# Input projection of a hybrid decoder layer on Trainium2: chunk-by-chunk start, paired chunk steps, conditioning by a pace per tile

## The chip, the core and the metric

The kernel runs on one core of one Trainium2 chip. A core has a matrix engine (PE, whose weight load is shown as PEld), a vector engine (DVE), a scalar engine (ACT), a general engine (POOL) and an engine whose queue issues nearly all transfers here (SP). The metric is the device time of one execution in microseconds (us): the median of three runs of the kernel before is 1449.34 us, the lowest 1449.11, the highest 1449.62. The profile is one further execution with its trace.

## The reference

One layer, one sequence of 256 positions, width 2048, all in 32-bit floats. A vector c conditions the layer: six vectors of 2048 (shift, scale and gate for each of two sub-layers) come from one product with a 2048 x 12288 matrix, `w_ada`.

```
c_act = silu(c)
mod = c_act @ w_ada + b_ada
sh1, sc1, g1, sh2, sc2, g2 = split(mod, 6)
h = layer_norm(x) * (1.0 + sc1) + sh1
y = token_mixer(h, w_in, ...)          # proj = h @ w_in, then attention and mLSTM
x = layer_norm(ALPHA * x + g1 * y, ...)
h = layer_norm(x) * (1.0 + sc2) + sh2
y = conv_ffn(h, w_up, ..., w_down)
x = layer_norm(ALPHA * x + g2 * y, ...)
```

Inside the token mixer one input projection `proj = h @ w_in` feeds two branches. One is a sparse attention with eight heads (compressed, selected and sliding-window keys, mixed by gates). The other is an mLSTM matrix memory with four heads, whose forget gates need a running maximum over all positions before it can start. Merge gates (another part of the projection, `mg`) mix the branches, an output projection follows, and then a gated feed-forward with a short convolution, which is most of the arithmetic. The change touches the layer norm and conditioning of x, the input projection, and the order of four small steps of the mLSTM and attention gates.

## The kernel before

**Products in three parts.** A 32-bit product is made of three products of a reduced type: the high part of both, and high by low in both orders. Every weight tile of 128 x 1024 floats (512 KB) is loaded by SP into one of 7 buffers `w`; ACT rounds it to its high part `wh` (L138), DVE subtracts to get the low part `wl` (L139), with 4 buffers each; then PE multiplies (L105). The activations are split in the same way into `hT` (high and low, L376 and L377).

**Row chunks and groups.** The 2048 rows of `w_in` are 16 row chunks k of 128, and PE accumulates over them in PSUM. They are taken in groups of 3, 4, 5 and 4 chunks. Within a group come first 24 blocks b of 128 columns (`ps_b`), then six column strips (`ps_a`, 392 or 512 wide). Eight of the blocks (0 to 7) stay in four PSUM banks over all groups; the others are added up in SBUF after each group. A weight tile holds 8 blocks of one chunk or two chunks of one strip, so a chunk takes six tiles and all 16 take 96. `order_b` gives the order of blocks and chunks within a group.

**Conditioning.** Chunk k can be used once its 128 shifts and scales are known: two dot products of 2048 with c, which DVE makes of transferred rows of `w_ada`, either one instruction of 128 x 2048 (L216, buffers `adaA`, `adaB`) or two of 128 x 1024 (L226, in `w` buffers), then two small additions into `modc` (L244, L245). Then ACT scales and shifts the normalised, transposed `nT` into `hm` (L374), casts `hT` high (L376), and DVE subtracts `hT` low (L377). A ticker hands out one conditioning product every few weight tiles, at a rate worked out per group so that the next group's chunks are through by then, and drains what is left at the group's end (`tk.drain`). Beyond the start, chunks are modulated two at a time.

**Startup.** x is normalised and transposed on PE (L353, `ps_nT`), ACT copies the transposes out of PSUM to `nT` (`turned`, L357), chunks 0 and 1 are conditioned together (`ada_mod(0, 2)`), then the first tile starts. Matmuls on zeros (L365, `ps_i`, 12 and then 4) stand among them on PE. DVE and ACT are ordered by hand in this part.

**Gate steps.** In the last group the generator `gate_steps` makes, step by step, the transposes and the small vector work for the branches: `ps_sT`, `ps_F`, `ps_uT` (L597, copied by DVE at L599, then a running maximum, the scan at L600, to `mT`), `ps_mc` (L604, transposes of `mT`), `ps_sc` (L615). Steps are taken between the tiles of strips 3 and 4 (at `(k - k0) % 2`, so four of them); what is left over is taken later in one go, in a block whose PE order is by hand and in which the matmuls of `ps_mg` stand before and after. All other order comes from a scheduler of the language that sets each engine's queue ahead of time; on the chip each engine works its queue in order.

Of the kernel before, what the change touches and what calls it, by code (L numbers as in the profile page):

```python
# [14 lines left out]
P = 128  # L15
# [17 lines left out]
GROUPS = (3, 4, 5, 4)  # L33
FIRST = 2
# [7 lines left out]
NIDLE = 12, 4  # L42
# [34 lines left out]
def build(ctx: ExitStack, tc: tile.TileContext, d, out, dbg=None):  # L77
# [54 lines left out]
    def load_split(src, off=0, t=None, after=()):  # L132

        n = src.shape[-1]
        if t is None:
            t = load(src)
        wh, wl = halves(off)
        hi = nc.scalar.copy(wh[:, :n], t[:, :n])  # L138
        lows.append(nc.vector.tensor_sub(wl[:, :n], t[:, :n], wh[:, :n]))  # L139
        for ins, other in zip((hi, lows[-1]), after):  # L140
            behind(ins, other)
        return wh, wl
# [56 lines left out]
    ring, cyclic, wide = [], [], []  # L199
# [33 lines left out]
    def ada_cols(m, n, k0, k1, then=None):  # L233
# [7 lines left out]
        def last():  # L241
# [3 lines left out]
            nc.vector.tensor_add(o, o, bada[:, m:m + n, k0:k1])  # L245
# [23 lines left out]
    class Ticker:  # L269
# [25 lines left out]
        def until(self, g):  # L295
            self.flush()
            while g in self.q:
                run_all(self.q.pop(0))
# [57 lines left out]
    def turned(p):  # L356
        return nc.scalar.copy(nT[:, 2 * p:2 * p + 2, :], psx.pop(p).rearrange("p (a b) -> p a b", a=2))  # L357
# [9 lines left out]
    def modulate_in(k0, k1):  # L367
        tmp = t2([P, 2, S], "hm")[:, :k1 - k0, :]
        for k in range(k0, k1):
            if k0 == 0:  # L370
                nc.vector.tensor_scalar(tmp[:, k - k0, :], nT[:, k, :], modc[:, 1, k:k + 1],
                                        modc[:, 0, k:k + 1], op0=ALU.mult, op1=ALU.add)
                continue
# [5 lines left out]
    mods = []  # L379

    def ada_mod(k0, k1):

        while k0 < k1:
            k = min(k0 + 2, k1)
            yield from ada_cols(0, 2, k0, k, lambda k0=k0, k=k: mods.append(modulate_in(k0, k)))
            k0 = k

    adaA = pg.tile([P, 2, D], F32, name="adaA", tag="gates0")
    ring += [None, None, adaA[:, 0, :]]
    zr = t2([P, 512], "zr", F32R)  # L390
    nc.gpsimd.memset(zr.bitcast(F32), 0.0)
    first = ada_mod(0, FIRST)
    idle(NIDLE[0], zr[:, :P], zr)
    with tc.manual_schedule(engines={mybir.EngineType.DVE, mybir.EngineType.Activation}):
# [6 lines left out]
        todo = [next(first) for _ in range(4)]  # L401
        tile0 = load(d["w_in_b"][0])
        steps = []
        for t in range(2):
            st = p0.tile([P, 4, 6], F32, name="st_x%d" % t, tag="st", bufs=2)
            for c in range(4):
                nc.vector.bn_stats(st[:, c, :], xt[:, t, c * 512:(c + 1) * 512])
                if t and c == 0:
# [3 lines left out]
                    for i in range(2):  # L412
# [4 lines left out]
        for i in range(2, 4):  # L417
            normalise(0, i)
# [3 lines left out]
        for f in todo[:1]:  # L422
            f()
# [3 lines left out]
        for f in todo[1:]:  # L427
            f()
        for c in range(2):
            normalise(1, c)  # L430
            for p in (2 * c, 2 * c + 1):
                turn(p, 1)
        turned(0)
        normalise(1, 2)
        turned(1)
        split0 = halves(OFFB[0])
        nc.scalar.copy(split0[0], tile0)
# [4 lines left out]
        for p in (2, 3):  # L442
            turned(p)
# [3 lines left out]
        for f in first:  # L447
            f()
        lows.append(nc.vector.tensor_sub(split0[1], tile0, split0[0]))
        for p in (4, 5):  # L450
            turned(p)

# [89 lines left out]
    def turn_rest():  # L542
        adaB = p0.tile([P, 2, D], F32, name="adaB", tag="t16")
        ring.extend([adaA[:, i, :] for i in range(2)] + [adaB[:, i, :] for i in range(2)])
        cyclic.append(1)
# [6 lines left out]
    def load_rest():  # L552
        nc.sync.dma_start(gb, d["ml_gate_b"][0:1, :].to_broadcast([P, 8]))
        nc.sync.dma_start(prm, d["prm"])
        msk = t2([P, P], "msk")
        nc.sync.dma_start(msk, d["msk"])
# [78 lines left out]
    def stream(src, width, per, off=0):  # L635

        for i in range(src.shape[0]):
# [3 lines left out]
            if n == 1:  # L641
                turn_rest()
            if n:
                t = load(cut, wide[-1] if n in (2, 3) else None)
                wh, wl = load_split(cut, off[i % 2], t, mods[n // 4] if n in (1, 4) else ())
                if n == 1:
                    for p in (6, 7):
                        turned(p)
            else:
                wh, wl = split0  # L650
            if n == 8:
                load_rest()
            if n in (1, 2):
                tk.tick(1.0)
                tk.flush()
            elif n:
                work()
            for i in range(per):
# [3 lines left out]
                                                           ("w_in_v", 512, 2, (0, 0))))  # L662
    k0 = 0
    lag = []
    for gi, kn in enumerate(GROUPS):
        nxt = gi < len(GROUPS) - 1
        if nxt:
            if gi == 0:
                tk.add(ada_mod(FIRST, kn))
            tk.add(ada_mod(k0 + kn, k0 + kn + GROUPS[gi + 1]))  # L670
            rate = 2 * GROUPS[gi + 1] / (6 * kn - (4 if gi == 0 else 2))
        else:
            rate = GR1
            ring.clear()
        comp = []

        def work():
# [3 lines left out]
            tk.tick(rate if nxt or c < 3 else GR2)  # L681

        c = 0
        for b, ks in order_b(gi):
# [870 lines left out]
```

## Time and profile before

| | |
|---|---|
| median of 3 runs | 1449.34 us (1449.11 to 1449.62) |
| profiled execution, its own time | 1448.23 us |
| its span, first to last instruction | 1446.3 us |
| mean granted PE clock | 0.994 |
| PE busy | 1418.9 us (98%) |
| DVE busy | 1061.5 us (73%) |
| ACT busy | 700.2 us (48%) |
| first matmul of each group | 25.02, 74.53, 140.64, 216.74 us |
| `ps_uT`, `ps_mc`, `ps_sc` | 293.47, 299.92, 300.13 us |

A row of the timeline gives the start, the time of the instructions in it, the engine, the line, the operation with its tiles, shapes, how many instructions the row joins, and in square brackets how long the engine was idle before and which instruction ended that. A row of the windows gives the stretch and its length, the busy time of PE, PEld, DVE, ACT and POOL in it with the number of instructions, the clock granted to PE as a share of full speed, the share of the transfer engines' time, and GB/s. A group row gives the number of instructions, their busy time, the mean ns of one, and the idle time before them.

### The profile page before, as it was taken

How to read it: one execution, taken by the hardware profiler on the slowest of the kernel's cores; microseconds unless marked ns; L12 is line 12 of the kernel's file. 1: busy time of each engine (PE TensorE's matmuls, PEld its weight loads, DVE VectorE, ACT ScalarE, POOL GpSimd, SP SyncE). 2: the span in 40 equal slices, each digit the busy share in tenths (PEclk: the TensorE clock that was granted, in tenths of full speed). 3: DMA queues.
4: the chain of work that ended last, by engine and by line, in shares of the span. 5: the costliest groups of instructions: out<-in, count | busy, mean ns of one | idle time of the engine just before them, and what ended most of it. 6: DMA issues, size and time to landing. Idle time of an engine off the chain costs nothing.

```text
span 1446.3 us, 23680 instructions
## 1 busy us (share of the span) xinstructions
PE 1418.9 (98%) x9361; PEld 1280.7 (89%) x9361; DVE 1061.5 (73%) x1486; ACT 700.2 (48%) x954; POOL 3.6 (0%) x10
## 2 busy tenths in 40 slices
PE   7999999999999999999999999999999999999996
PEld 6998998877777888888999999988889999998886
DVE  7889886888787898779878768755555555555566
ACT  5654344746566444445565454444334444444341
POOL 0000000000000000000000000000000000000000
PEclk8999999999999999999999999999999999999998
DMA  9999878886867999899188878866666666666661
GB/s 373 418 403 371 286 239 279 301 289 217 308 219 288 357 318 344 342 334 349 37 298 293 289 237 287 292 191 190 189 198 195 192 195 196 192 193 197 190 205 59
DMA packets 103183, 374.25 MB, mean 259 GB/s; under 512 B 11168, under 2 KB 11680, under 8 KB 102304
## 3 DMA queue, kind: packets, MB, share of 16 engines
q1 hardware_dynamic: 103072, 372.75, 75.3%
q8 instruction: 73, 1.20, 0.3%
q14 instruction: 38, 0.31, 0.1%
HBM read 370.61 MB, written 2.10 MB: 258 GB/s over the span
## 4 chain that ended last, share of the span: by engine, by line
PE 89%; DVE 6%; ACT 2%; issue 1%; DMA 1%; DVEq 0%
PE ps_up L105 33%; PE ps_d L105 17%; PE ps_mg L105 12%; PE ps_b L105 8%; PE ps_br L105 6%; PE ps_a L105 6%; PE ps_o L105 3%; DVE wl L139 2%; PE ps_s L105 1%; PE ps_y L105 1%; PE ps_hid L105 1%; DVE w L226 1%; DVE adaB L216 1%; DVE xz L1150 0%; DMA w<-in_w_o_dram 0%
## 5 line engine op out<-in xcount | busy, mean ns | idle before, releaser
L139 DVE TENSOR_TENSOR wl<-w,wh 128x1024 fp32r<-128x1024 f32 (+1 forms) x475 | 571.0, 1206 | 321.7 <-ACT wh L138 320.4
L138 ACT CAST wh<-w 128x1024 fp32r<-128x1024 f32 (+1 forms) x475 | 490.9, 1038 | 610.2 <-PE ps_up L105 184.9
L105 PE MATMUL ps_up<-h2T,wh 128*128 128x256 f32 x2816 | 480.9, 276 | 0.5 <-DVE h2T L1258 0.5
L105 PEld LDWEIGHTS ps_up<-h2T,wh 128*128 128x128 f32 x2816 | 424.4, 188 | 0.9 <-DVE h2T L1258 0.8
L105 PE MATMUL ps_up<-h2T,wl 128*128 128x256 f32 x1408 | 386.8, 276 | 0.0
L105 PEld LDWEIGHTS ps_up<-h2T,wl 128*128 128x128 f32 x1408 | 264.4, 188 | 0.0
L105 PE MATMUL ps_d<-wh,uTt 128*128 128x512 f32 (+1 forms) x704 | 205.6, 376 | 0.0
L105 PE MATMUL ps_mg<-wh,hT 128*128 128x512 f32 x512 | 169.2, 401 | 0.0
L226 DVE SCALAR_TENSOR_TENSOR w<-w,crow 128x1024 f32<-128x1024 f32 x134 | 163.0, 1219 | 3.0 <-ACT crow L197 3.0
L105 PEld LDWEIGHTS ps_d<-wh,uTt 128*128 128x128 f32 x704 | 129.2, 188 | 24.0
L105 PE MATMUL ps_b<-hT,wh 128*128 128x256 f32 x768 | 133.7, 282 | 1.5 <-ACT hT L376 1.2
L105 PE MATMUL ps_d<-wl,uTt 128*128 128x512 f32 (+1 forms) x352 | 132.2, 376 | 0.0
L105 PEld LDWEIGHTS ps_b<-hT,wh 128*128 128x128 f32 x768 | 115.6, 190 | 5.7 <-issue 3.3
L105 PEld LDWEIGHTS ps_mg<-wh,hT 128*128 128x128 f32 x512 | 96.2, 188 | 22.6 <-issue 3.1
L105 PE MATMUL ps_a<-wh,hT 128*128 128x392 f32 (+1 forms) x384 | 108.4, 359 | 0.0
L105 PE MATMUL ps_b<-hT,wl 128*128 128x256 f32 x384 | 101.2, 279 | 0.7 <-DVE wl L139 0.7
L105 PE MATMUL ps_mg<-wl,hT 128*128 128x512 f32 x256 | 100.0, 391 | 0.0
L105 PEld LDWEIGHTS ps_a<-wh,hT 128*128 128x128 f32 x384 | 70.8, 188 | 7.2 <-issue 2.1
L105 PEld LDWEIGHTS ps_d<-wl,uTt 128*128 128x128 f32 x352 | 66.1, 188 | 11.9
L105 PE MATMUL ps_a<-wl,hT 128*128 128x392 f32 (+1 forms) x192 | 69.6, 362 | 2.3 <-DVE wl L139 2.3
L105 PEld LDWEIGHTS ps_b<-hT,wl 128*128 128x128 f32 x384 | 69.7, 188 | 1.7 <-DVE wl L139 1.3
L105 PE MATMUL ps_o<-wh,mgT 128*128 128x512 f32 (+1 forms) x208 | 62.3, 381 | 0.0
(278 smaller groups left out, 1280.7 us busy)
## 6 DMA issues: line engine op xcount, KB each, us to landing
w<-in_w_up_dram SPq DMA_DIRECT2D x176, 512.0 KB, 4.3
w<-in_w_ada_dram SPq DMA_DIRECT2D x134, 512.0 KB, 4.7
w<-in_w_down_dram SPq DMA_DIRECT2D x89, 512.0 KB, 3.7
w<-in_w_mg_dram SPq DMA_DIRECT2D x64, 512.0 KB, 5.0
w<-in_w_in_b_dram SPq DMA_DIRECT2D x48, 512.0 KB, 7.0
w<-in_w_br_dram SPq DMA_DIRECT2D x32, 512.0 KB, 5.2
w<-in_w_o_dram SPq DMA_DIRECT2D x32, 512.0 KB, 5.4
adaA<-in_w_ada_dram SPq DMA_DIRECT2D x15, 1024.0 KB, 10.9
```

Of the source, the lines that this page charges most:

```text
L105: nc.tensor.matmul(o, lhsT, rhs, start=start, stop=stop)
L138: hi = nc.scalar.copy(wh[:, :n], t[:, :n])
L139: lows.append(nc.vector.tensor_sub(wl[:, :n], t[:, :n], wh[:, :n]))
L216: ins = nc.vector.scalar_tensor_tensor(t, t, 1.0, crow, op0=ALU.mult, op1=ALU.mult, accum_out=parts[:, row(m), k, 0:1])
L226: ins = nc.vector.scalar_tensor_tensor(t, t, 1.0, crow[:, i * 1024:(i + 1) * 1024], op0=ALU.mult, op1=ALU.mult, accum_out=parts[:, row(m), ...
```

## The change

- **Startup, chunk by chunk.** Chunk 0 is conditioned and modulated alone, straight out of PSUM by ACT (`modulate_one`), then chunk 1, then chunk 2. The first four weight tiles are opened by hand (`high`, `low`, `opened`): the order on PE is now written out too, with transposes of later chunks between the first tiles' matmuls. Nine instead of four idle matmuls stand before it.
- **Order of blocks.** Group 0 takes blocks 8 to 15 and 0 to 7 of chunk 0, the same of chunk 1, then of chunk 2. Later groups take the 16 blocks in steps of two chunks. Blocks 16 to 23 follow whole.
- **Conditioning.** One table `PACE` by the number of the tile gives the pace; nothing is drained at a group's end. Where a chunk is needed that isn't modulated yet, `need` forces what is queued.
- **Others.** The loads of three constants move from tile 8 to tile 46; the second ring buffer `adaB` is set up before the first group. In the last group the ring is cleared at block 3, not ahead of the group.
- **Gate steps.** They are taken in strips 3 and 4 at `(k - k0) % 3 == 2`: one per strip instead of two. The other three go to the block with the order by hand.

```diff
+PACE = ((26, 0.51), (42, 0.25), (50, 0.5), (72, 0.3), (96, 0.5))
-NIDLE = 12, 4
+NREST = 46
+NIDLE = 12, 9
...
-    if gi == len(GROUPS) - 1:
-        return [(b, range(kn)) for b in range(NBLK)]
-    most = 2 * HELD + (0 if gi else 8)
-    a, z = range(FIRST), range(FIRST, kn)
-    first = [*range(2 * HELD, most), *range(2 * HELD)]
-    return ([(b, a) for b in (range(most) if gi else first)] + [(b, z) for b in range(2 * HELD, most)]
-            + [(b, z) for b in range(2 * HELD)] + [(b, range(kn)) for b in range(most, NBLK)])
+    held, free = range(2 * HELD), range(2 * HELD, 2 * HELD + 8)
+    pairs = [range(k, min(k + 2, kn)) for k in range(0, kn, 2)]
+    if gi:
+        parts = [(ks, g) for ks in pairs for g in (held, free)]
+    else:
+        parts = [([k], g) for ks in ((0, 1), (2,)) for g in (free, held) for k in ks]
+    return [(b, ks) for ks, g in parts for b in g] + [(b, range(kn)) for b in range(16, NBLK)]
...
+        def force(self):
             self.flush()
-            while g in self.q:
-                run_all(self.q.pop(0))
+            f = next(self.q[0], 1)
+            if f == 1:
+                self.q.pop(0)
+            elif f:
+                f()
...
+    def modulate_one(k, src):
+        tmp = t2([P, S], "hm1")
+        for o in (hT[:, k, 0, :], tmp):
+            nc.scalar.activation(o, src, AF.Identity, bias=modc[:, 0, k:k + 1], scale=modc[:, 1, k:k + 1])
+        return lambda: nc.vector.tensor_sub(hT[:, k, 1, :], tmp, hT[:, k, 0, :])
...
+        todo[1]()
+        normalise(1, 0)
+        turn(0, 1)
+        late = modulate_one(0, psx[0][:, :S])
+        opened(0, 0, 8, 0, 0)
+        low(0)
+        late()
+        normalise(1, 1)
         turned(0)
+        opened(0, 0, 8, 1, 0)
+        opened(0, 0, 8, 0, 1)
+        for p in range(1, 4):
+            turn(p, 1)
+        sums[0]()
+        ring += adas
...
+        opened(1, 1, 8, 0, 0)
+        low(1)
+        later[0]()
+        high(2)
+        turned(3)
+        opened(1, 1, 8, 1, 0)
+        opened(1, 1, 8, 0, 1)
...
-            if n == 8:
+            if n == NREST:
                 load_rest()
...
+    def need(k):
+        while ready[-1] <= k:
+            tk.force()
...
-            rate = 2 * GROUPS[gi + 1] / (6 * kn - (4 if gi == 0 else 2))
-        else:
-            rate = GR1
-            ring.clear()
+        rate = None
...
-            tk.tick(rate if nxt or c < 3 else GR2)
+            pace = next(r for n, r in PACE if tiles[0] <= n)
+            tk.tick((rate or pace) if nxt or c < 3 else GR2)
...
             for k in ks:
+                need(k0 + k)
...
-                if not nxt and c in (3, 4) and (k - k0) % 2:
+                if not nxt and c in (3, 4) and (k - k0) % 3 == 2:
                     next(steps)
...
-        if nxt:
-            tk.drain()
```

In the order rows below a name after the operation is what is written and, behind the arrow, what is read; numbers at the end of a row count equal instructions in a row.

**PE at the start.** `ps_i` are the idle matmuls, `ps_nT` the transposes of x, `ps_b` the first blocks. Before:

```order
L365 MATMUL ps_i<-zr 128x512 x12
L353 MATMUL ps_nT<-head,xt 128x128 x8
L365 MATMUL ps_i<-zr 128x512 x4
L353 MATMUL ps_nT<-head,xt 128x128 x24
L105 MATMUL ps_b<-hT,wh 128x256 x16
L105 MATMUL ps_b<-hT,wl 128x256 x8
```

With the change:

```order
L372 MATMUL ps_i<-zr 128x512 x12
L358 MATMUL ps_nT<-head,xt 128x128 x8
L372 MATMUL ps_i<-zr 128x512 x9
L358 MATMUL ps_nT<-head,xt 128x128 x2
L107 MATMUL ps_b<-hT,wh 128x256 x8
L107 MATMUL ps_b<-hT,wl 128x256 x8
L107 MATMUL ps_b<-hT,wh 128x256 x8
L358 MATMUL ps_nT<-head,xt 128x128 x14
L107 MATMUL ps_b<-hT,wh 128x256 x8
L107 MATMUL ps_b<-hT,wl 128x256 x8
L107 MATMUL ps_b<-hT,wh 128x256 x8
L358 MATMUL ps_nT<-head,xt 128x128 x8
```

Ten transposes stand ahead of the first block instead of 32; the other 22 stand behind the first and the second tile.

**DVE in the same part, with the change,** from the last product of chunk 0 to the first of chunk 2 (`hm_229` and `hm_286` are chunks 0 and 1):

```order
L228 SCALAR_TENSOR_TENSOR w,parts<-w,crow 128x1024
L246 TENSOR_TENSOR modc<-parts 128x2
L247 TENSOR_TENSOR modc<-modc,head 128x2
L417 TENSOR_TENSOR wl<-w,wh 128x1024
L386 TENSOR_TENSOR hT<-hm_229,hT 128x256
L218 SCALAR_TENSOR_TENSOR adaA,parts<-adaA,crow 128x2048 x2
L246 TENSOR_TENSOR modc<-parts 128x2
L247 TENSOR_TENSOR modc<-modc,head 128x2
L417 TENSOR_TENSOR wl<-w,wh 128x1024
L386 TENSOR_TENSOR hT<-hm_286,hT 128x256
L218 SCALAR_TENSOR_TENSOR adaA,parts<-adaA,crow 128x2048
```

Each chunk has its own products, sums and low half here, and low halves of weight tiles stand between them; before, chunks 0 and 1 came together. Both products of chunk 1 are now 128 x 2048 and stand behind the low half of chunk 0. Chunk 2 follows in the same way, with the low halves of two tiles between its sums and its own low half.

**PE and DVE at the gate steps.** `ps_uT`, `ps_mc` and `ps_sc` are the three transposes, `ps_mg` the matmuls around them. PE with the change:

```order
L107 MATMUL ps_mg_3100<-wh,hT 128x512
L107 MATMUL ps_mg_3100<-wl,hT 128x512
L107 MATMUL ps_mg_3100<-wh,hT 128x512
L655 MATMUL ps_uT<-head,sm 4x128 x2
L662 MATMUL ps_mc<-head,mT 128x4 x2
L673 MATMUL ps_sc<-head,scT 128x128 x4
L107 MATMUL ps_mg_3099<-wh,hT 128x512
```

Before, three matmuls of `ps_a` and 24 of `ps_mg` stood between `ps_uT` and `ps_mc`; now none. DVE with the change, in the same place:

```order
L141 TENSOR_TENSOR wl<-w,wh 128x1024 x2
L228 SCALAR_TENSOR_TENSOR w,parts<-w,crow 128x1024
L657 COPY uT<-ps_uT 4x256
L141 TENSOR_TENSOR wl<-w,wh 128x1024
L228 SCALAR_TENSOR_TENSOR w,parts<-w,crow 128x1024
L658 SCALAR_TENSOR_TENSOR mT<-uT 4x256
```

One low half and one conditioning product stand between the copy of `uT` and the scan that makes `mT`, which the transposes into `ps_mc` read.

More of the change, by code (lines that the diff above doesn't have):

```diff
@@ L139, in load_split @@
         lows.append(nc.vector.tensor_sub(wl[:, :n], t[:, :n], wh[:, :n]))
-        for ins, other in zip((hi, lows[-1]), after):
-            behind(ins, other)
+        if after:
+            behind(lows[-1], after)
         return wh, wl
@@ L384, in ada_mod, with one_mod, high, low @@
             k = min(k0 + 2, k1)
-            yield from ada_cols(0, 2, k0, k, lambda k0=k0, k=k: mods.append(modulate_in(k0, k)))
+            yield from ada_cols(0, 2, k0, k, lambda k0=k0, k=k: (modulate_in(k0, k), ready.append(k)))
             k0 = k
     adaA = pg.tile([P, 2, D], F32, name="adaA", tag="gates0")
-    ring += [None, None, adaA[:, 0, :]]
+    adas = [adaA[:, i, :] for i in range(2)]
+    ring += [None, None, *adas]
     zr = t2([P, 512], "zr", F32R)
     nc.gpsimd.memset(zr.bitcast(F32), 0.0)
-    first = ada_mod(0, FIRST)
+    later = []
+    def one_mod(k, low=lambda f: f()):
+        yield from ada_cols(0, 2, k, k + 1, lambda: (low(modulate_one(k, nT[:, k, :])), ready.append(k + 1)))
+    first, second, third = ada_cols(0, 2, 0, 1), one_mod(1, later.append), one_mod(2)
+    splits = [halves(OFFB[i % 2]) for i in range(4)]
+    begun = [None] * 5
+    for j in range(HELD, HELD + 4):
+        psb[j] = bank(psm, "ps_b")
+    def high(n):
+        nc.scalar.copy(splits[n][0], begun[n])
+    def low(n):
+        lows.append(nc.vector.tensor_sub(splits[n][1], begun[n], splits[n][0]))
+    def opened(n, k, b0, w, x):
+        for i in range(8):
+            b = b0 + i
+            mm(psb[b // 2][:, (b % 2) * S:(b % 2 + 1) * S], splits[n][w][:, i * P:(i + 1) * P], hT[:, k, x, :],
+               not (k or w or x or b % 2), False)
     idle(NIDLE[0], zr[:, :P], zr)
-    with tc.manual_schedule(engines={mybir.EngineType.DVE, mybir.EngineType.Activation}):
+    with tc.manual_schedule(engines={mybir.EngineType.DVE, mybir.EngineType.Activation, mybir.EngineType.PE}):
         todo = [next(first) for _ in range(2)]
@@ L400, in build @@
             f()
-        todo = [next(first) for _ in range(4)]
-        tile0 = load(d["w_in_b"][0])
+        todo = [next(first) for _ in range(2)]
+        begun[0] = load(d["w_in_b"][0])
+        sums = [next(second) for _ in range(2)]
+        for n in range(1, 5):
+            begun[n] = load(d["w_in_b"][n])
         steps = []
@@ L416, in build @@
             steps.append(g)
-        for i in range(2, 4):
-            normalise(0, i)
+        normalise(0, 3)
+        high(0)
         for p in range(4):
@@ L426, in build @@
         nmr(mvx[1])
[L427 to L432, printed above, removed]
-        turned(0)
+        todo[1]()
[6 more added lines that the diff above has]
+        normalise(1, 1)
+        turned(0)
+        opened(0, 0, 8, 1, 0)
[4 more added lines that the diff above has]
+        ring += adas
+        sums.append(next(third))
         normalise(1, 2)
+        high(1)
         turned(1)
-        split0 = halves(OFFB[0])
-        nc.scalar.copy(split0[0], tile0)
         normalise(1, 3)
@@ L446, in build @@
                 turn(p, t)
[L447 to L450, printed above, removed]
+        for p in range(4, 8):
             turned(p)
+            psb[p - 4] = bank(psa, "ps_b")
+        sums[2]()
+        sums.append(next(third))
+        high(3)
+        low(2)
+        opened(2, 0, 0, 0, 0)
+        opened(2, 0, 0, 0, 1)
+        opened(2, 0, 0, 1, 0)
+        low(3)
+        opened(3, 1, 0, 0, 0)
+        opened(3, 1, 0, 0, 1)
+        opened(3, 1, 0, 1, 0)
+        sums[3]()
     ast = ExitStack()
@@ L540, in dest_b @@
         return accM[:, 2 * i - 16:2 * i - 14, :], None
[L542 to L545, printed above, removed]
+    adaB = p0.tile([P, 2, D], F32, name="adaB", tag="t16")
+    ring += [t[:, i, :] for i in range(2) for t in (adaA, adaB)]
+    cyclic.append(1)
     gsig = pa.tile([P, 2, 24], F32, name="gsig")
@@ L712, in build @@
                 if not nxt and b == 3:
+                    ring.clear()
+                    rate = GR1
                     comp.append(compress())
```

63 lines of the change are left out of this document (22 added, 41 removed).

## The prediction

> **What bounds the kernel now.** I read the chain of waits on the page first, then the windows by group, then the timeline around the places that the change touches.
>
> ```profile
> PE 89%; DVE 6%; ACT 2%; issue 1%; DMA 1%; DVEq 0%
> ```
>
> ```profile
> 25.00:74.50 49.50, 48.48 (x324) 45.75 (x325) 43.90 (x47) 28.92 (x44) 0.00 (x0) 0.97 1.03 418
> 74.50:140.60 66.10, 63.69 (x433) 59.42 (x432) 62.21 (x76) 29.76 (x37) 0.00 (x0) 1.00 0.99 385
> 140.60:216.70 76.10, 76.10 (x541) 73.74 (x541) 64.48 (x75) 34.07 (x39) 0.00 (x0) 1.00 0.78 270
> 216.70:299.90 83.20, 83.20 (x629) 69.89 (x628) 64.12 (x104) 46.34 (x63) 1.37 (x2) 1.00 0.83 287
> ```
>
> The four windows are the four groups of row chunks, the last one cut at the transposes of the gate steps. PE is busy without a gap in groups 2 and 3. Group 2 does 5 chunks in 76.10 us, so a chunk costs 15.2 us of PE. At that rate groups 0 and 1 (7 chunks) would need 106.5 us; they take 49.5 + 66.1 = 115.6. So 9.1 us is all that better conditioning and a better start of the blocks can win there, apart from the start itself. DVE is the rival engine: 43.90 of 49.50, then 62.21 of 66.10. From the gate steps on, the order of PE is the same in both kernels to the end, so whatever the change does is decided before, and what PE gains or loses by then is carried to the end one to one, since PE waits for little after it.
>
> **The start.** The first block's matmul comes at 25.02:
>
> ```profile
> 14.93 1.82 PE L365 MATMUL ps_i<-zr 128*128 128x512 f32 x4
> 17.01 1.22 DVE L226 SCALAR_TENSOR_TENSOR w<-w,crow 128x1024 f32<-128x1024 f32 x1
> 18.00 3.67 PE L353 MATMUL ps_nT<-head,xt 128*128 128x128 f32 x16 [1.25 <-ACT xt L344]
> 21.51 1.22 DVE L226 SCALAR_TENSOR_TENSOR w<-w,crow 128x1024 f32<-128x1024 f32 x1
> 22.97 0.17 DVE L245 TENSOR_TENSOR modc<-modc,head 128x4 f32<-128x4 f32 x1
> 24.34 0.63 ACT L376 CAST hT<-hm 128x512 fp32r<-128x512 f32 x1
> 25.02 0.51 PE L105 MATMUL ps_b<-hT,wh 128*128 128x256 f32 x2 [1.20 <-ACT hT L376]
> ```
>
> It waits for `modc` of both chunks, whose last product begins at 21.51 and whose sums end at 23.14, 1.63 us later. Chunk 0's own products are done with the one that begins at 17.01, so its sums would end at 17.01 + 1.63 = 18.64. Nine idle matmuls at 1.82 / 4 = 0.46 us would end at 14.93 + 4.1 = 19.0 at worst; I take 18.7, since the 0.46 holds a tail that is paid once. Two transposes and one ACT pass over 128 x 256 follow. That pass costs:
>
> ```profile
> 36.19 0.60 ACT L374 ACTIVATE hm<-nT,modc 128x256 f32<-128x256 f32 x1 [3.69 <-DVE modc L245]
> ```
>
> So the first block's matmul comes at 18.7 + 0.45 + 0.6 = 19.75: **5.3 us earlier**. The 22 transposes that now stand behind it cost PE time after that point: 3.67 / 16 = 0.23 us each at half clock, 0.115 at full, **2.5 us**.
>
> **What the early start meets.** PE now waits for one chunk after the other. I walk the queues with these rows:
>
> ```profile
> 25.75 3.30 PE L105 MATMUL ps_b<-hT,wh 128*128 128x256 f32 x14 [0.22 <-DVE hT L377]
> L139 DVE TENSOR_TENSOR wl<-w,wh 128x1024 fp32r<-128x1024 f32 x94 | 114.0, 1220 | 33.5 <-ACT wh L138 32.7
> L138 ACT CAST wh<-w 128x1024 fp32r<-128x1024 f32 x94 | 97.7, 1052 | 100.5 <-PE ps_b L105 33.9 <-PE ps_mg L105 22.1 <-PE ps_a L105 21.0
> L216 DVE SCALAR_TENSOR_TENSOR adaA<-adaA,crow 128x2048 f32<-128x2048 f32 x15 | 34.3, 2284 | 0.8 <-DMA adaA<-in_w_ada_dram 0.8
> 37.27 0.43 DVE L377 TENSOR_TENSOR hT<-hm,hT 128x256 fp32r<-128x256 f32 x1 [1.17 <-ACT hT L376]
> ```
>
> Tile 0 takes 24 matmuls, at 3.30 / 14 = 0.236 half clock or 0.118 full, 2.8 us; with 14 transposes (1.6) PE is through at 24.1. DVE makes the low half of tile 0, then of chunk 0 (till about 20.8), then both products of chunk 1 (2 x 2.28), the sums (0.4), and ACT its pass (0.6): 26.35. PE waits **2.2 us**. Chunk 2 has the same form, with two low halves of tiles (1.22 each) ahead of its own in DVE's queue: **1.9 us**. The banks of PSUM that `turned` must free, and small waits, I put at **0.8**. In group 1 the second pair of chunks has its low half behind the low half of a tile: **1.0**. In group 2 the cast of the second pair's `hT` stands in ACT's queue behind the cast of a tile three ahead, which needs a `wh` buffer that PE frees only when it reaches the pair: 1.05 + 0.62 + a semaphore, **1.8**. These sum to 7.7 us in groups 0 to 2, against 9.1 before.
>
> Group 3 would begin at 19.75 + 12 x 15.2 + 2.5 + 7.7 = 212.35, instead of 216.74 before: **-4.4 us**. Without one of these waits but the two at the start it would be -8.0; with all waits half as long again, -0.5. That no product is drained at a group's end costs nothing by itself: the 29 long products are spread out, DVE's 2.28 us each lie beside PE's 15.2 a chunk, and DVE's share falls to about 93% in every group. The constants' loads at tile 46 fall where the transfer engines are at 0.78. In group 3 ring and compression begin three tiles later; a wait of ACT for its own queue there I put at **+0.6** (0 to 1.2, one cast's 1.05 being the nearest row).
>
> **The gate steps.** This is the edit that costs. Before:
>
> ```profile
> 293.47 0.38 PE L597 MATMUL ps_uT<-head,sm 128*4 128x128 f32 x2
> 295.08 0.69 DVE L734 TENSOR_TENSOR projA<-ps_a,projA 128x512 f32<-128x512 f32 x1
> 295.68 0.40 DVE L599 COPY uT<-ps_uT 4x256 f32<-4x256 f32 x1
> 296.01 0.67 DVE L734 TENSOR_TENSOR projA<-ps_a,projA 128x512 f32<-128x512 f32 x1
> 296.61 1.20 DVE L139 TENSOR_TENSOR wl<-w,wh 128x1024 fp32r<-128x1024 f32 x1
> 297.75 0.67 DVE L600 TENSOR_TENSOR_SCAN mT<-uT 4x256 f32<-4x256 f32 x1
> 299.54 1.22 DVE L226 SCALAR_TENSOR_TENSOR w<-w,crow 128x1024 f32<-128x1024 f32 x1
> 299.92 0.28 PE L604 MATMUL ps_mc<-head,mT 4*128 4x4 f32 x2
> ```
>
> From the end of `ps_uT` (293.85) to the end of the scan (298.42) are 4.6 us, which 27 matmuls on PE cover; PE shows no gap. With the change nothing stands between `ps_uT` and `ps_mc`, and PE works its queue in order, so it must stand while DVE does copy (0.40), low half (1.20), product (1.22) and scan (0.67): 3.5 us. The low half also needs its high half from ACT, which starts once PE frees the buffer; I take **4.1 us**. Below 3.5 it can't go with this order of DVE; above, 5.9, if DVE is as far behind at the copy as before (295.68 against 293.85). Nothing later waits more for it, and `ps_mg` is all that PE has queued behind.
>
> **The clock.** A gap on PE may cost more than itself:
>
> ```profile
> 8.40:11.80 3.40, 1.95 (x9) 1.25 (x7) 3.33 (x9) 0.60 (x2) 0.00 (x0) 1.00 1.03 400
> 11.80:15.20 3.40, 1.34 (x9) 1.11 (x10) 3.23 (x11) 1.69 (x3) 0.00 (x0) 1.00 1.03 422
> 15.20:18.60 3.40, 2.15 (x7) 1.27 (x6) 3.29 (x9) 3.00 (x5) 0.00 (x0) 0.50 1.03 420
> 22.00:25.40 3.40, 1.52 (x10) 1.14 (x10) 2.20 (x7) 3.14 (x8) 0.00 (x0) 1.00 0.99 365
> 25.40:28.85 3.45, 3.23 (x16) 3.11 (x15) 2.65 (x3) 1.49 (x3) 0.00 (x0) 0.51 1.03 420
> 412.68 1.13 PE L105 MATMUL ps_y<-pT,projA 128*128 128x512 f32 x2 [1.43 <-ACT pT L803]
> ```
>
> The granted clock (third column from the right) changes in steps of 3.4 us. A step with PE busy 1.34 or 1.52 us is followed by one at half clock; a wait of 1.43 us inside busy work (412.68) is not. A gap of 4.1 us leaves at least one step at 0 to 1.7 us busy, so one step at half clock follows, and half of its 3.4 us of work is lost: **+1.6** (0 to 2.5). The change gains one such step at the start (25.40 to 28.85, where nine idle matmuls now fill the step before), which is in the first block's earlier end, not counted again.
>
> [...]
>
> **The sum.** -4.4 + 0.6 + 4.1 + 1.6 = +1.9 us. The profiled execution took 1448.23 us for a span of 1446.3, and would take 1450.1; the runs' median lies 1.1 above it, so I predict 1449.34 + 1.9 = **1451.2 us**. A difference within 0.2% (2.9 us) is about what a measurement of this kernel can't tell from none.
>
> **Rivals.**
>
> *The gain stays (0.25).* The gate steps' wait is partly paid by DVE's lead, the clock stays up, and the waits in groups 1 and 2 do not appear: PE starts group 3 at -7.2 instead of -4.4 (1.0 and 1.8 less), and the gates cost 3.5. For it: groups 2 and 3 ran without a gap before with DVE at 64.48 of 76.10. Against: the order shows the casts behind each other. -7.2 + 0.6 + 3.5 = -3.1, **1446.2 us**.
>
> *The clock falls at the short waits too (0.16, slower).* One mechanism: a step of 3.4 us in which PE is busy under some 1.5 to 1.9 us is followed by half clock. The waits of 2.2 us at 24.1 to 26.35 and of 1.9 us at chunk 2 leave 1.2 to 1.5 if they fall into one step, and the gates' gap can touch two steps. Each costs 1.7; three more make 5.1 less the share of waits that a slower PE hides (about 1.0): 1451.2 + 4.1 = **1455.3 us**. It decides from a wait of about 1.9 us in one step on. For it: the two steps quoted. Against: a step with 1.95 busy (8.40 to 11.80) kept its clock.
>
> *The early start gains nothing (0.14).* The transfers run at 418 GB/s with a share of 1.03 in group 0, so chunk 2's rows and the tiles may come no earlier; then PE waits out all 4.4 and the change is 0 + 0.6 + 4.1 + 1.6 = +6.3, **1455.6 us**. Against: the spread of conditioning takes bytes out of groups 0 and 1.
>
> **How the numbers follow.** The forecast has 0.45, with 0.02 of it faster, 0.35 the same and 0.08 slower; its own range is 1448 to 1454.5 (the gates' wait and clock at their ends, one of the smaller waits missing). Of the first rival's 0.25, 0.21 is faster and 0.04 the same; of the second's 0.16, 0.02 the same and 0.14 slower; of the third's, 0.02 and 0.12. Faster 0.23, same 0.43, slower 0.34. The range reaches down to 1444.5 (the first rival with the clock term 0 and 1.7 less of waits at the start) and up to 1456.5 (the third rival with one more step at half clock half paid).
>
> **What would show it.** Right: first `ps_b` within half a us of 19.75; a PE wait of about 2 us for ACT's chunk 1 pass before the second tile; group 3 at 211 to 214; a PE gap of 3.5 to 5 us ahead of `ps_mc`, released by DVE's scan, followed by a step at half clock. Wrong: if group 3 begins before 209.5 the waits in groups 1 and 2 were not there; if after 215 the start was eaten; if no gap shows before `ps_mc`, the queue's order was not what decides.

## The result

The changed kernel takes 1458.34 us (median of 6 runs, 1454.85 to 1463.27) against 1449.22 (6 runs, 1448.55 to 1449.68) for the kernel before: a ratio of 1.0064, 95% interval 1.0051 to 1.0077. It is slower by 9.1 us, outside the predicted range of 1444.5 to 1456.5. Five more runs of the unaltered change, taken later, had a median of 1457.66. All eleven lie between 1454.85 and 1463.27; so the change scatters over 8 us, where the kernel before scatters over 1.1 us in these six runs and over 4.4 (1447.19 to 1451.55) in the 23 taken beside runs 5 to 8. The profiled execution happened to be the longest, 1463.27 us with a span of 1461.5; another, profiled later, has a span of 1454.3. Both are needed below.

The windows of the changed kernel by group, in the first profile (the last one ends behind the gate transposes):

```profile
19.28:76.44 57.16, 52.34 (x346) 49.22 (x347) 45.46 (x50) 36.91 (x57) 0.00 (x0) 0.97 1.01 404
76.44:138.62 62.18, 61.35 (x433) 59.25 (x432) 57.77 (x68) 28.21 (x33) 0.00 (x0) 1.00 0.93 360
138.62:221.00 82.38, 79.30 (x541) 76.54 (x540) 70.91 (x84) 33.59 (x38) 0.00 (x0) 0.96 0.81 287
221.00:314.10 93.10, 86.58 (x636) 73.12 (x634) 68.66 (x113) 50.59 (x68) 1.37 (x2) 0.96 0.80 271
```

The first block comes at 19.28, 5.7 us earlier than before. Group 0 then takes 57.16 us (49.5 before) and gives it all back; group 1 takes 62.18 (66.1 before), group 2 82.38 (76.1), and the last takes 92.5 us from its first block to `ps_sc` (83.4 before). PE had no gap in groups 2 and 3 before; now it is 3.1 and 6.5 us short of the window, and its clock is 0.96 in both. What PE waited for between 19 and 320 us (engine, tile and line, engine and tile it waited for, us in total, times, longest):

```profile
PE ps_mc L662 <- DVE mT L658: 3.9, 1, 3.9
PE ps_b L107 <- ACT hT L385: 2.6, 3, 1.3
PE ps_b L107 <- DVE hT L380: 2.3, 2, 1.5
PE ps_a L107 <- ACT wh L140: 2.1, 1, 2.1
PE ps_b L107 <- ACT hT L379: 1.6, 1, 1.6
PE ps_b L107 <- DVE wl L417: 1.5, 1, 1.5
PE ps_b L107 <- DVE hT L386: 1.2, 1, 1.2
```

Most of these are the waits that the prediction named: the scan at the gates (3.9), the passes and low halves of chunks 1 and 2 (L385, L386), the cast of `hT` in group 2 (L379). Three are not: the low half of `hT` in group 2 (1.5 of the 2.3 of L380), the strip of v (`ps_a` for `wh`, 2.1), and the low half of a weight tile in group 0 (L417, 1.5). The rows shown sum to 15.2 us, and to 15.9 with two smaller ones; the same view of the kernel before sums to 5.4:

```profile
PE ps_a L105 <- DVE wl L139: 2.3, 7, 0.5
PE ps_b L105 <- ACT hT L376: 1.2, 1, 1.2
PE ps_nT L353 <- ACT nT L357: 1.0, 1, 1.0
PE ps_b L105 <- DVE wl L139: 0.7, 2, 0.5
PE ps_b L105 <- DVE hT L377: 0.2, 1, 0.2
```

The longest wait before was 1.2 us; seven of the change's are longer than 1. That is not only more waiting. The steps of 3.4 us in which three of them fall, each with the step behind it (the third column from the right is the granted clock):

```profile
149.84:153.26 3.42, 1.20 (x8) 1.00 (x8) 3.42 (x4) 1.48 (x2) 0.00 (x0) 1.00 0.90 329
153.26:156.67 3.41, 2.60 (x12) 2.61 (x13) 1.41 (x5) 1.01 (x2) 0.00 (x0) 0.50 1.02 414
282.96:286.38 3.42, 1.33 (x9) 0.89 (x8) 0.65 (x1) 1.71 (x2) 0.00 (x0) 1.00 1.01 406
286.38:289.79 3.41, 2.88 (x8) 2.20 (x8) 2.74 (x6) 3.35 (x6) 0.00 (x0) 0.50 0.70 227
310.27:313.69 3.42, 0.43 (x4) 0.41 (x5) 3.04 (x5) 0.39 (x2) 0.00 (x0) 1.00 0.87 289
313.69:317.10 3.41, 3.41 (x11) 2.83 (x10) 2.71 (x9) 2.13 (x5) 0.00 (x0) 0.50 0.79 315
```

PE busy 1.20, 1.33 and 0.43 us of 3.4, and half clock in the next step. After the first two, PE was busy 2.60 and 2.88 us in that step, and the half clock held for a second one (153.26 to 160.09, 286.38 to 293.20).

### The profile page after: what moved, and what is told of

Read it like the earlier page. It is cut to its first block, busy times and chain, and to the rows that moved or that the text cites. A ratio compares the mean times of both kernels' runs of the same rounds, so it can differ in the third digit from the quotient of the medians.

```text
span 1461.5 us, 23701 instructions
## 1 busy us (share of the span) xinstructions
PE 1424.0 (97%) x9366; PEld 1288.1 (88%) x9366; DVE 1061.6 (73%) x1485; ACT 704.2 (48%) x958; POOL 3.6 (0%) x10
## 4 chain that ended last, share of the span: by engine, by line
PE 90%; DVE 5%; DMA 2%; ACT 1%; issue 1%; SPq 0%; DVEq 0%; ACTq 0%
PE ps_up L107 33%; PE ps_d L107 16%; PE ps_mg L107 12%; PE ps_b L107 8%; PE ps_a L107 8%; PE ps_br L107 6%; PE ps_o L107 3%; DVE wl L141 1%; PE ps_s L107 1%; PE ps_y L107 1%; DMA w<-in_w_in_b_dram 1%; DVE w L228 1%; PE ps_hid L107 1%; DMA adaA<-in_w_ada_dram 1%; DVE xz L1196 0%
## 5 line engine op out<-in xcount | busy, mean ns | idle before, releaser
L107 PEld LDWEIGHTS ps_d<-wl,uTt 128*128 128x128 f32 x352 | 66.1, 188 | 11.9
```

What stands on the lines that cost most here:

```text
L107: nc.tensor.matmul(o, lhsT, rhs, start=start, stop=stop)
```

## The gate steps

PE and DVE at the gate steps in the changed kernel, from the timeline:

```profile
308.97 0.38 PE L655 MATMUL ps_uT<-head,sm 128*4 128x128 f32 x2
313.26 0.28 PE L662 MATMUL ps_mc<-head,mT 4*128 4x4 f32 x2 [3.91 <-DVE mT L658]
...
309.82 0.41 DVE L657 COPY uT<-ps_uT 4x256 f32<-4x256 f32 x1
310.25 1.23 DVE L141 TENSOR_TENSOR wl<-w,wh 128x1024 fp32r<-128x1024 f32 x1
311.39 1.22 DVE L228 SCALAR_TENSOR_TENSOR w<-w,crow 128x1024 f32<-128x1024 f32 x1
312.53 0.67 DVE L658 TENSOR_TENSOR_SCAN mT<-uT 4x256 f32<-4x256 f32 x1
```

DVE takes the copy 0.47 us behind the transposes (309.82 against 309.35), then low half, product and scan without a break. From transposes to transposes PE does 0.2 us of work in 4.3.

**Run 1: the kernel before with the gate steps of the change alone.**

```diff
-                if not nxt and c in (3, 4) and (k - k0) % 2:
+                if not nxt and c in (3, 4) and (k - k0) % 3 == 2:
```

> The kernel before with one edit: gate steps taken at every third chunk (one per strip) as in the change, so that the transposes of uT, mc and sc stand back to back on PE. Theory A (PE's wait is paid in full, and a step at half clock follows): a gap of about 4.1 us ahead of ps_mc and 1.7 us of half clock behind it, 1449.2 + 5.8 = 1455.0 us. Rival B (DVE or the transfers set the pace there and PE only waits in another place): no change, 1449 us. Rival C (the wait counts, the clock doesn't fall): 1453.3 us.

Measured: 1455.18 us (5 runs, 1453.21 to 1456.87) against 1449.03; ratio 1.0044 (1.0031 to 1.0056). The only wait of PE between 280 and 320 us is this one, and half clock follows it:

```profile
PE ps_mc L604 <- DVE mT L600: 3.9, 1, 3.9
...
302.47:305.88 3.41, 0.87 (x7) 0.86 (x8) 3.01 (x7) 0.82 (x3) 0.00 (x0) 1.00 0.83 284
305.88:309.30 3.42, 3.42 (x9) 2.66 (x9) 2.77 (x10) 1.71 (x3) 0.00 (x0) 0.50 0.82 313
```

One line of the change costs 6.2 us by itself, as theory A had it (5.8): two thirds of the whole loss.

**Run 2: the change, with real work between uT and mc.**

```diff
-        fill(2, GR2)
+        fill(1, GR2)
+        next(steps)
+        fill(2, GR2)
         for _ in steps:
             pass
-        fill(2, GR2)
+        fill(1, GR2)
```

> The changed kernel with two of the four tiles of ps_mg that stand around the gate steps put between uT and mc (24 matmuls, 5.4 us of work). Nothing else moves. Theory A: the gap of 4.1 us ahead of ps_mc and the half-clock step behind it are gone, 1458.3 - 5.8 = 1452.5 us, and the runs spread less. Rival B: 1458 us, the wait turns up elsewhere. Rival C: 1454.2 us.

Measured: 1451.62 us (11 runs, 1448.91 to 1452.63), 6.7 us below the change (6.0 below the median of its later five runs). Expected were 5.8. The 24 matmuls cover the whole wait, and nothing waits for it later.

**Run 3: the change, with idle matmuls there.** The wait for the scan stays; PE is only kept busy in it.

```diff
         fill(2, GR2)
+        next(steps)
+        ps = bank(psa, "ps_i")
+        for i in range(16):
+            tc.keep_in_program_order(nc.tensor.matmul(ps, hT[:, 0, 0, :P], hT[:, 0, :, :], start=True, stop=True))
         for _ in steps:
```

> The changed kernel with 16 idle matmuls (3.6 us of PE, results not used) between uT and mc. The wait for the scan stays as it is, only PE is busy in it. Theory A (the clock falls where PE stands for more than about half of a 3.4 us step): ps_mc comes at the same distance behind uT, no half-clock step behind it, 1458.3 - 1.7 = 1456.6 us. Rival C (the clock has no part in the time): 1458.3 us, or later if the idle matmuls outlast the wait.

Measured: 1454.32 us (5 runs, 1453.06 to 1455.25), 4.0 us below the change's first median, 3.3 below that of its later runs. PE's timeline in this run:

```profile
301.10 0.38 PE L655 MATMUL ps_uT<-head,sm 128*4 128x128 f32 x2
301.23 3.89 PE L1023 MATMUL ps_i<-hT 128*128 128x512 f32 x16
305.39 0.28 PE L662 MATMUL ps_mc<-head,mT 4*128 4x4 f32 x2 [0.27 <-DVE mT L658]
...
301.33:304.74 3.41, 3.41 (x18) 2.80 (x16) 3.39 (x7) 1.01 (x1) 0.00 (x0) 1.00 0.90 293
304.74:308.15 3.41, 3.14 (x17) 2.39 (x16) 2.65 (x8) 2.33 (x5) 0.00 (x0) 1.00 0.94 342
```

`ps_mc` comes 4.29 us behind `ps_uT`, to the hundredth as in the change (313.26 - 308.97). No half clock follows. Work whose result nobody reads makes the kernel faster: the clock has a share, and rival C (the clock has no part) falls. The gain is larger than the 1.7 us I expected. The change's second profile shows one reason:

```profile
300.62:304.04 3.42, 0.67 (x4) 0.20 (x3) 3.40 (x6) 1.04 (x1) 0.00 (x0) 1.00 0.95 340
304.04:307.45 3.41, 2.25 (x9) 2.04 (x10) 2.64 (x8) 2.10 (x4) 0.00 (x0) 0.50 1.00 364
```

The gap of 4.1 us touches two steps. The second has 1.2 us of it, and PE is busy 2.25 us at half clock; the clock stayed at half for one step more (304.04 to 310.87). So at the gates the clock costs, by an estimate from these rows, 1.7 us in the first profile (half of the 3.41 us busy in its one step at half clock) and 2.8 in the second ((3.41 - 1.2) / 2 + 1.7). From `ps_sc` to the end the traces have 1147.99 us (first profile), 1148.78 (second) and 1146.41 (run 3), so 1.6 and 2.4 us. What the 3.3 to 4.0 us have beyond that is not shown; it may be half-clock steps in other places, of which the trace of run 3 has none from its first block on (mean clock 0.996, against 0.989 and 0.993 in the change's two profiles).

## The second pair of group 2, and the scatter

**Run 4** belongs to the next section. **Run 5: conditioning earlier.**

```diff
-PACE = ((26, 0.51), (42, 0.25), (50, 0.5), (72, 0.3), (96, 0.5))
+PACE = ((26, 0.51), (42, 0.32), (50, 0.5), (72, 0.3), (96, 0.5))
```

> The changed kernel with one number of the pace table raised (0.25 to 0.32 for tiles 26 to 42), so that the second pair of chunks of group 2 is conditioned some two tiles earlier, and the loads and casts around it shift with it. Theory A (PE waits 1.6 us for the cast of hT and 1.5 for its low half there, and half clock follows in some executions): both gaps near 150 us go, 1458.3 - 3.4 - 0 to 3.4 = 1451.5 to 1455 us, middle 1454. Rival B (DVE is the bound of groups 1 and 2; the wait moves to group 1): 1458 us, new gaps between 76 and 138 us.

Measured: 1452.08 us (11 runs, 1449.9 to 1454.18), 6.3 us below the change (5.6 below its later runs), more than the 4.3 that the middle of theory A had. Both waits near 150 us are gone, and group 3 begins at 212.44 instead of 221.00 (217.31 in the change's second profile); no new wait of over 1.0 us stands between 76 and 212. Rival B (the wait moves to group 1) falls for this step.

What those two waits were, in the change's first profile:

```profile
149.75 1.04 ACT L140 CAST wh<-w 128x1024 fp32r<-128x1024 f32 x1 [0.72 <-ACT hm L377]
150.71 0.61 ACT L379 CAST hT<-hm 128x512 fp32r<-128x512 f32 x1
151.37 1.20 PE L107 MATMUL ps_b<-hT,wh 128*128 128x256 f32 x8 [1.58 <-ACT hT L379]
152.20 1.21 DVE L141 TENSOR_TENSOR wl<-w,wh 128x1024 fp32r<-128x1024 f32 x1
153.34 0.67 DVE L380 TENSOR_TENSOR hT<-hm,hT 128x512 fp32r<-128x512 f32 x1
154.06 0.58 PE L107 MATMUL ps_b<-hT,wh 128*128 128x256 f32 x1 [1.50 <-DVE hT L380]
```

The cast of `hT` stands behind the cast of a weight tile, as the prediction said (1.58). Then DVE, in its own order, makes the low half of that tile (1.21) before the low half of `hT`, and PE stands again after eight matmuls (1.50). The second wait follows from DVE's order in the same way and was not counted.

**Run 9: the change once more, unaltered.**

> The changed kernel once more, unaltered. Theory A (its waits of 1.6 to 4.1 us leave the clock up or down by how the free-running 3.4 us steps happen to fall on them): the time scatters again by 5 us or more between executions, 1454 to 1463 us, longer where the mean granted clock is lower, by 1.7 us for each half-clock step; the waits themselves are the same in the trace. Rival (the long times of the first profile came from something else that the profiled executions shared): times within 1 us of each other.

Measured: 1457.66 us (5 runs, 1456.37 to 1459.8): a scatter of 3.4 us, less than the 5 expected, and more than the 1 us that the rival wanted. The waits near 150 us are the same in this trace (1.6 and 1.5), the clock is not:

```profile
147.02:150.44 3.42, 1.91 (x17) 1.71 (x16) 3.42 (x3) 2.70 (x5) 0.00 (x0) 1.00 0.92 352
150.44:153.85 3.41, 1.86 (x13) 1.66 (x14) 2.95 (x6) 0.41 (x2) 0.00 (x0) 1.00 1.00 396
```

Here the border of two steps falls between the waits: 1.91 and 1.86 us busy, and the clock stayed full in the step behind them too. In the first profile both fell into one step (1.20), and half clock held from 153.26 to 160.09: 3.0 us of work lost, half of the 2.60 and 3.41 us that PE was busy in those two steps. The waits are the program's; what they cost went with the place of the steps, whose borders near them the same program had at 149.84 and 153.26 in one execution and at 147.02 and 150.44 in the other. Counted in half-clock steps from the first block to 320 us the first profile has six (one near 41, two at 153 to 160, two at 286 to 293, one at 314) and the second three (one near 34, two at 304 to 311). Of the 7.2 us between their spans, 1.1 arise in group 0, 2.8 in group 2 and 4.3 in the last group up to `ps_sc`; the second gives back 0.3 by a later first block and 0.8 behind `ps_sc`. The 4.3 also hold the strip-of-v wait of 2.1 us that the second trace lacks, less one of 0.9 that only the second has. That the scatter of the other nine executions has the same cause is not shown. Their mean clocks only hint at it: 0.994 in the two shortest executions and 0.989 in the longest, but 0.993 in the second longest (1459.8).

## The last group

**Run 4: the last group's blocks in the order of before.**

```diff
+    if gi == len(GROUPS) - 1:
+        return [(b, range(kn)) for b in range(NBLK)]
```

> The changed kernel with the last group's blocks in the order of the kernel before (each block over all four chunks), so that compression begins after two or three tiles instead of five. Theory A (compression's weights hold the w buffers three tiles longer, the loads of the strip of v are issued late, PE waits 2.1 + 0.5 us at its first tile, and half clock follows): these waits go, 1458.3 - 2.6 - 1.7 to 3.4 = 1452.3 to 1454.0 us. Rival B (the order of blocks has no part; the load is late because of the transfers): 1458 us.

Measured: 1455.78 us (5 runs, 1454.44 to 1458.7), 2.6 us below the change, 1.9 below its later runs; expected were 4.3 to 6. Between 200 and 320 us PE now waits only at the gates. So the order of the blocks does cause the waits in group 3. What they cost is not settled: the runs overlap with those of the change, and from the first block of group 3 to `ps_uT` run 4 takes 83.8 us, the change 88.0 in its first profile but 83.6 in its second. In the first profile PE stood 2.1 us for the first tile of v:

```profile
284.65 1.04 ACT L140 CAST wh<-w 128x1024 fp32r<-128x1024 f32 x1 [3.39 <-DMA w<-in_w_in_v_dram]
```

The load was issued at 277.57; before, at 267.70, so it came 9.9 us later where the group had begun only 4.3 later. In the second profile this wait is missing, and only one of 0.9 us for the compression's gelu (`ps_vc` for `gT`) is there. Why the load was so late in one execution I did not settle; that compression's weights hold `w` buffers longer is an argument from the queue of loads, in which it and the strip's loads alternate.

## The start

For the walk through group 0 the exact order of blocks matters. The code (`order_b` and the calls of `opened`) takes blocks 8 to 15 of chunk 0, then the same blocks of chunk 1, then blocks 0 to 7 of chunk 0 and of chunk 1, and then chunk 2. So PE needs chunk 1 right behind the first tile, as the prediction's walk has it.

**Run 6: everything but the start.** The sixth kernel is the kernel before with the pace table, `need`, the paired chunk steps from group 1 on, the loads at tile 46 and the gate steps of the change; startup and group 0 stay as they were.

```diff
...
-    if gi == len(GROUPS) - 1:
-        return [(b, range(kn)) for b in range(NBLK)]
+    if gi:
+        held, free = range(2 * HELD), range(2 * HELD, 2 * HELD + 8)
+        pairs = [range(k, min(k + 2, kn)) for k in range(0, kn, 2)]
+        return [(b, ks) for ks in pairs for g in (held, free) for b in g] + [(b, range(kn)) for b in range(16, NBLK)]
...
+                need(k0 + k)
...
-        if nxt:
-            tk.drain()
```

> All of the change but its start: startup and group 0 in the manner of the kernel before (chunks 0 and 1 together, then chunk 2), with the pace table, need, paired chunk steps from group 1 on, loads at tile 46 and gate steps of the change. Theory D (the first block comes 5.5 us earlier, and group 0 gives all of it back: 22 transposes, four waits for chunks 1 and 2): group 1 begins at about 74.5 us as before, 1457 to 1458.3 us. Rival (the start is worth what the first block gains): 1463 us.

Measured: 1458.34 us (5 runs, 1455.87 to 1458.5), the same as the change. A first block at 25.71 instead of 19.28 costs nothing in the whole, and group 1 begins at 74.36 here, earlier than in run 2 (74.90), whose trace has the new start and no half-clock step in group 0 (mean clock 0.996). Part of the equal time is a coincidence: in this run PE waits 4.0 us near 150 (2.7 for the cast of `hT`, 1.3 for its low half), 0.9 more than in the change, so the comparison does not weigh the start alone.

**Run 7: the three edits of runs 2, 4 and 5 together, with the start of the change.**

> The changed kernel with the edits of the second (ps_mg between uT and mc), fourth (last group's blocks whole) and fifth run (pace 0.32) together. Theory A (each wait named is paid in full and independently): 1451.6 (second run) - 3.4 at the second pair of group 2 - about 1.3 in group 3 - 0.5 of half clock = 1446.4 us, faster than the kernel before by 2.6 us. Rival B (waits that are taken away come back): 1449 to 1451 us.

Measured: **1444.82 us** (7 runs, 1444.51 to 1446.17); ratio to the kernel before 0.9973 (0.9963 to 0.9984). It beats both kernels, by 4.3 us (1449.11 beside it) and 13.5 us, and is 1.6 us below theory A's forecast. Its windows by group:

```profile
20.02:75.14 55.12, 51.01 (x347) 47.68 (x348) 45.35 (x50) 37.47 (x57) 0.00 (x0) 1.00 1.02 407
75.14:137.67 62.53, 61.70 (x437) 59.54 (x436) 58.81 (x70) 27.99 (x33) 0.00 (x0) 1.00 0.97 383
137.67:213.03 75.36, 75.36 (x538) 72.99 (x536) 70.43 (x86) 35.10 (x41) 0.00 (x0) 1.00 0.86 301
213.03:299.49 86.46, 86.46 (x642) 72.34 (x640) 66.43 (x108) 47.08 (x63) 1.37 (x2) 1.00 0.82 282
```

PE has no gap in groups 2 and 3, and in this execution the clock is full from the first block on. The scatter is 1.7 us. The edits alone gave 6.7, 2.6 and 6.3 us, in sum 15.6; together 13.5. So the waits are nearly independent, and none that was taken away came back elsewhere; rival B, which had them come back, falls.

**Run 8: the same three edits on the sixth kernel.**

> The same three edits on the sixth run's kernel (start of the kernel before, all else of the change). Theory D (the start gives nothing by group 1): within 1 us of the seventh run, 1446.4 us, and with less spread, since no waits stand between 24 and 40 us. Rival (the start keeps part of its gain): 1449 to 1451 us.

Measured: 1447.15 us (11 runs, 1445.47 to 1450.23); ratio 0.999 (0.9981 to 0.9998). It is 2.3 us slower than run 7, so what differs at the start is worth 2.3 us; theory D had expected less than 1. Its runs also spread more (4.8 us against 1.7), where less was expected. But the traces do not show that these 2.3 us are a part of the first block's lead that lasts. The first block comes 4.75 us earlier in run 7 (20.02 against 24.77), group 1 only 0.8 (75.14 against 75.96), although run 8 has a half-clock step in group 0 (33.80 to 37.22) and run 7 has none (mean clocks of the two executions 0.995 and 0.996). Group 3 begins 3.1 us earlier (213.03 against 216.16), so most of the lead arises anew in groups 1 and 2, where run 8 waits 0.9 us for a low half of `hT` among others; what else differs there is open. Up to group 1, then, theory D is nearly right, and group 0 shows what eats the lead. It takes 55.12 us in run 7, 49.50 before (with a half-clock step in them): some 2.5 of the 5.6 are the 22 transposes (by the prediction's estimate of 0.115 us each), and PE stands for 4.1 of the 55.12 (1.0 before). One of these waits was not foreseen. DVE's first product of chunk 2 stood for its transfer:

```profile
29.82 2.29 DVE L218 SCALAR_TENSOR_TENSOR adaA<-adaA,crow 128x2048 f32<-128x2048 f32 x1 [3.21 <-DMA adaA<-in_w_ada_dram]
32.03 2.36 DVE L417 TENSOR_TENSOR wl<-w,wh 128x1024 fp32r<-128x1024 f32 x2
33.31 1.19 PE L107 MATMUL ps_b<-hT,wl 128*128 128x256 f32 x8 [1.48 <-DVE wl L417]
```

The low halves of two weight tiles stood behind that product in DVE's queue, though the high half of the first was done at 27.09, and PE stood behind them. The rows are from the change's first profile. From 16.7 to 33.8 us the transfers carried 369 to 420 GB/s, about what group 0 carried before (418).

**Run 10: run 7 with the first pace raised too.**

```diff
-PACE = ((26, 0.51), (42, 0.32), (50, 0.5), (72, 0.3), (96, 0.5))
+PACE = ((26, 0.58), (42, 0.32), (50, 0.5), (72, 0.3), (96, 0.5))
```

> The seventh run's kernel with the pace of the first 26 tiles raised from 0.51 to 0.58, so that the second pair of chunks of group 1 is conditioned a tile earlier. Theory A: the gap of 1.0 us near 86 us goes, and nothing takes its place: 1444.8 - 1.0 = 1443.8 us. Rival B (group 0 and 1 are at DVE's and the transfers' bound; the earlier products delay low halves of tiles): 1444.8 to 1446 us, with new gaps between 50 and 86 us.

Measured: 1449.88 us (11 runs, 1448.14 to 1451.79), 5.1 us slower than run 7; theory A (a gain of 1.0) is wrong here. The gap at 86 us is gone, and these are the longest rows in the view of PE's waits (the second had 2.4 in run 7, the others had 0.5 and nothing):

```profile
PE ps_b L109 <- DVE wl L143: 3.1, 3, 2.2
PE ps_b L109 <- ACT hT L387: 2.9, 3, 1.8
PE ps_b L109 <- ACT wh L142: 1.8, 1, 1.8
```

The low halves and the high halves of weight tiles are late now. In group 2 there was room for earlier products (run 5); in groups 0 and 1 there is none. Rival B is right about these two groups, but said 1444.8 to 1446, too little, and looked for the new gaps between 50 and 86 us; they stand before 48 and after 86. A half-clock step at 47.34 comes on top (mean clock 0.994, in run 7 0.996).

**Run 11: run 7 with four idle matmuls.**

```diff
-NIDLE = 12, 9
+NIDLE = 12, 4
```

> The seventh run's kernel with four instead of nine idle matmuls ahead of the first block. Theory A (a step in which PE is busy for less than about 1.8 us is followed by half clock, and the nine keep one such step from the start): the first tiles run at half clock for one or two steps in most executions, but part of it lies where PE waits for chunk 1 anyway: 1444.8 + 0.5 to 2.5, middle 1446.3 us. Rival (the idle matmuls only delay the first transposes): 1444.8 us or 0.5 less.

Measured: 1444.39 us (7 runs, 1443.89 to 1446.04), as run 7 within the scatter: the rival is right and theory A (1446.3) is not. The clock does fall, behind a step in which PE was busy 0.97 us (11.49 to 14.90), but the time does not mind:

```profile
14.90:18.31 3.41, 2.49 (x9) 1.57 (x7) 3.27 (x10) 3.08 (x5) 0.00 (x0) 0.50 1.03 422
```

PE is at half speed (0.50 in each of three steps) until 25.14, through the first tile and the transposes behind it, and then stands for chunk 1 as before, only a shorter time (busy 2.38 of 3.41 us from 25.14 to 28.55). The nine idle matmuls buy nothing here, since what follows waits for DVE.

## Why the prediction was wrong, step by step

- **First block at 19.75:** 19.28, right to half a us. The tail in the 0.46 us of an idle matmul shows in rows of equal shape at full clock: 0.39 us for one, 0.62 for two (308.52 and 308.06 in the change's first profile).
- **Chunk 1 in 2.2 us, chunk 2 in 1.9, the second pair of group 1 in 1.0:** right. The gaps are 0.2 and 1.3 for chunk 1, 0.5 and 1.2 for chunk 2 and 0.8 for the pair. Counted from the start of one matmul to the start of the next, less the usual distance, they cost 2.0, 2.0 and 1.0 us in run 2.
- **"Banks and small waits, 0.8":** too small. The wait behind the transfer of chunk 2's rows (1.5, in run 2 1.2) was missed; it is the third rival's mechanism in a small place. Counted as above, group 0 loses some 6.7 us to waits in run 2, where the walk has 4.9. Without half-clock steps group 1 begins at 74.9 (run 2), not at the 72.7 that the walk gives (19.75 + 3 x 15.2 + 2.5 + 4.9).
- **The second pair of group 2, 1.8:** the cast was right, the low half behind it (1.5) was left out. The semaphore in the 1.8 was an estimate; the matmul begins 0.05 us behind the end of the cast (151.37 against 151.32). DVE's order was read for the gates but not for this place.
- **Group 3 at 212.35:** with these two, 216.56 (run 2). The gain of 4.4 us at that point was 0.2. This is the largest mis-sized term, 4.2 us, without any help from the clock.
- **Group 3, +0.6:** waits of 0.9 to 2.6 us in the six traces with this order of blocks; their cost is open, see run 4.
- **Gate steps, 4.1 + 1.6:** right. 3.9 us idle, 4.29 from `ps_uT` to `ps_mc` with some 0.2 of work in them, and 6.2 with the clock in run 1.
- **The clock at the short waits:** this was the slower rival, with 0.16, and by the sum below it lifts the time from about 1456 to 1458; it also makes the two profiles differ. Its price (1.7 us, half of a step of 3.41), its point (PE busy under 1.5 to 1.9 us in a step: 1.75 in the change's first profile, at 37.20, was followed by half clock, 1.83 in run 2 was not) and its places (start, chunk 2, the gates over two steps) were right, but the pair in group 2, where it cost 3.0 in the first profile, was not among them: one wait of 1.8 leaves a step some 1.6 us busy, between the 1.52 (before, at 22.00) and the 1.75 that both brought half clock. The error was to forecast the clock at one place and leave the others as a rival, when every one of them was near its point.

For the sum: -0.2 by group 3, about +1 there, +4.1 and +1.7 at the gates make 6.6. The median's remaining 1.8 to 2.5 us would be one to two half-clock steps; that is argued from the two profiles, not shown for the median. So the step that failed first is the walk to group 3, which put 7.7 us of waits into groups 0 to 2, where run 2 shows 4.2 more. No run varies the constants' loads, the second ring buffer or the ring's clearing alone.

The steps in these rows are 3.41 us long, and in one profile their borders lie whole steps apart: from 153.26 to 286.38 and on to 313.69 in the change's first profile are 39 and 8 steps of 3.413. In its second profile they lie elsewhere (147.02, where the first has 149.84). In the first, two gaps of 1.58 and 1.50 us in one step brought two steps at half clock (0.50).

## What to carry to other kernels

PE worked its queue in order here: with two dependent small steps set back to back it stood 3.91 us while matmuls of `ps_mg` were queued behind them, and the second came 4.29 us behind the first. So look at what stands between such steps in PE's queue, and at what stands ahead of their vector work in the other queue. Count a short wait twice where two fall into one step as here: once for itself (1.58 and 1.50 us), and once for the clock, which cost another 3.0 us in the first profile and nothing in the second, where a border lay between the two. These places made the two profiles differ; that other scatter is a sign of the like was not shown. A pace table that was a little early in one stage was worth 6.3 us (run 5) and in another cost 5.1 (run 10), so it is moved one entry at a time. An earlier first instruction was worth only what the queues behind it let through: a first block 4.75 us earlier brought group 1 forward by 0.8 (runs 7 and 8).

## What was not expected of the hardware

- The clock fell after steps that were not idle but busy for about half of their 3.41 us or less. At full clock, the steps in which PE was busy 0.43, 1.20, 1.33 and 1.75 us (the change's first profile, the last at 37.20), 0.67 (its second), 0.87 (run 1), 0.71 (run 5, at 296.79), 0.97 (run 11) and 1.34 and 1.52 (before) were each followed by half clock; those of 1.83 and 1.94 (run 2, below), 1.86 and 1.91 (the change's second profile) and 1.95 (before) were not. Whether one border lies between them is not shown. Once at half clock, a step with 2.60 or 2.88 us busy was followed by a second one at 0.50, so such a place cost some 3 us, an estimate (half of 2.60 or 2.88 and of 3.41).

```profile
147.04:150.45 3.41, 1.83 (x16) 1.63 (x15) 3.41 (x3) 1.84 (x3) 0.00 (x0) 1.00 1.00 380
150.45:153.87 3.42, 1.94 (x17) 1.74 (x16) 2.28 (x7) 1.01 (x2) 0.00 (x0) 1.00 0.98 371
```

- Sixteen matmuls whose result is not read made the kernel 3.3 to 4.0 us faster (run 3), with `ps_mc` as late behind `ps_uT` as without them.
